# First layer of a hybrid mixer block: queries and keys of the second attention are normed and rotated beside the first attention; inner products of the modulation come later

## The chip, the cores and the metric

One NeuronCore of one Trainium2 chip. The metric is the device time of one execution in microseconds (us); less is better. The engines that matter are PE (TensorE, matmuls and transposes), DVE (VectorE), ACT (ScalarE), POOL (GpSimd, which also starts some DMAs) and SP (which starts the DMAs of weights). Each engine takes its instructions in the order in which the program issued them; between engines only data and buffers order the work.

## The reference, cut to what matters

Two layers over 256 latent and 256 context tokens of width 1024. Each layer normalises and modulates the tokens, multiplies by one wide input matrix, runs three mixers on slices of the result (an mLSTM "ML", a grouped-query attention "GA" with normed and rotated queries and keys, and a neighbourhood attention "NA"), projects, gates and adds them, and ends in a ConvFFN. The second attention's part:

```python
def rms_norm(x, g):
    xf = x.astype(jnp.float32)
    y = xf * lax.rsqrt(jnp.mean(xf * xf, axis=-1, keepdims=True) + EPS)
    return (y * g.astype(jnp.float32)).astype(x.dtype)

def apply_rope(x, cos, sin):
    x1, x2, x3, x4 = jnp.split(x, 4, axis=-1)
    rot = jnp.concatenate([-x2, x1, -x4, x3], axis=-1)
    return x * cos[:, None, :] + rot * sin[:, None, :]

def gqa_qkv(zq, zk, zv, g_q, g_k):          # 8 query heads, 2 key heads of 64
    q = rms_norm(zq.reshape(B, T, GQA_HEADS, HEAD_DIM), g_q)
    k = rms_norm(zk.reshape(B, T, GQA_KV_HEADS, HEAD_DIM), g_k)
    ...

# in reference(), per layer:
mod = (jax.nn.silu(c) @ w_mod[l] + b_mod[l])[:, None, :]
sh1, sc1, ga1, sh2, sc2, ga2 = jnp.split(mod, 6, axis=-1)
...
y_ga = gqa_latent(apply_rope(q_a, cos, sin), apply_rope(k_a, cos, sin), v_a, kc_a, vc_a)
...
x = x + ga1 * rms_norm(o, g_post_mix[l])
f = conv_ffn(modulate(rms_norm(x, g_pre_ffn[l]), sh2, sc2), w_up[l], conv_w[l], conv_b[l], w_down[l])
x = x + ga2 * rms_norm(f, g_post_ffn[l])
```

Only latent tokens are rotated; context keys and queries are normed only. In the second layer the context rows' queries are not needed.

## The kernel before, in words

The kernel is one long list `prog` of pieces. A piece is one chunk of a weight matrix (2 x 128 rows by up to 512 columns) and the matmuls that use it. SP loads the chunk into one of five `raw` buffers; ACT casts it to a high part `whi` (L201), DVE subtracts to get the low part `wlo` (L205), and PE runs three matmul products, high by high and the two crossed ones (L319). `run` goes through the list: a chunk is split up to two pieces ahead of its matmuls, then the piece's matmuls are issued, then `side` steps (one as a rule, two for some pieces) of a queue of Python generators.

These side generators hold everything that isn't a weight matmul, cut at each `yield` into a step. A step's instructions lie on the engines' queues behind the matmuls of its piece. In order, within a layer:

- `g_na` (NA attention) and `g_gqa` (GA attention) end in `g_attend`, which runs in units: a step issues the value matmuls of unit t-2 (L717; ACT casts `yhi` L720, DVE subtracts `ylo` L721), the transposes of unit t-1 (L703, copied to `pT`) and the score matmuls of unit t (L664 for context units, L667 for latent ones), whose softmax DVE and ACT do (L676 to L686).
- ahead of its units, `g_gqa` has nine steps in each layer: the rotation tables (L778, L784); sums of squares and the reciprocal root (L793 to L799, twelve small DVE instructions L117 to L123); then seven steps in which `stage1` (norm and rotation of one 128-token tile: DVE L808, POOL L812 for context and L819 for latent tiles, and one step later DVE L824 and L826) and, three steps behind it, `stage2` (transposes L845 and L850, copies L847 and L851) are staggered. Keys are written twice side by side into a tile `kd`.
- `g_gates` (five steps): gate sums, POOL builds the matrices `GN` (L897 to L900), PE transposes them (L907, L908), later products with the sums L918 to L934.
- `g_mlstm` (mLSTM): `mrow` rows go to DRAM (L949) and come back broadcast as `mb` (L969, function `bcast`), ACT takes exponentials of them (`expo`, L998), DVE multiplies them into score products (L1015), PE forms the outputs (L1028).

PSUM has four banks for weight matmuls and four for side steps. A piece's `need` can force a generator to its end (`finish`).

The order of pieces around the change, layer 0: nq, nk, nv (behind which `g_na` joins the queue), the 272 columns of keys, values and gates (tile `akv`), the GA queries `aq` (piece `attend`, behind which `g_gqa`, `g_gates` and the mLSTM generators join), eight pieces zg(NA), four proj(NA) with two side steps each, eight zg(GA), mk, proj(GA), mq, mv, mo, zg(ML), proj(ML). In layer 1 the order is zg(NA), zg(GA), proj(NA), mk, mq, mv, proj(GA), mo. DVE's evacuation of a projected gate branch, `sig` (L1186), comes at the end of each projected half, with POOL's part L1193 in the later branches.

Between these stand dot pieces (`mod_dot`): one 512 KB chunk of `w_modT` each, which DVE multiplies with the conditioning vector and sums (L451, twice a chunk in layer 0, for latents and context), no PE work and no side step. `spread(a, b, list)` deals such pieces out evenly between two places of `prog`. In layer 0, sixteen of them (`sh2`, `sc2`) lie between `attend` and the last piece of proj(GA) and eight (`ga1`) behind it.

Line numbers in the text and the profile are those of the kernel before.

Of the kernel before, what the change touches and what calls it, by code (L numbers as in the profile page):

```python
# [8 lines left out]
F32 = mybir.dt.float32  # L9
# [4 lines left out]
ALU = mybir.AluOpType  # L14
# [23 lines left out]
class Piece:  # L38
    def __init__(self, raw, emit, k0=0, kn=0, split=True, pre=None, side=1, need=None, share=None, dot=False):
        self.raw, self.emit, self.k0, self.kn, self.split = raw, emit, k0, kn, split  # L40
        self.pre, self.side, self.need = pre, side, need
        self.hi = self.lo = None
        self.dot = dot
        self.hold = self.fence = False
        self.share = share
        if raw:
            raw.left += 1


class Builder:  # L50
# [115 lines left out]
    def run(self):  # L166
        nc = self.nc
        prog = self.prog
        raws = []
        for p in prog:  # L170
            if p.raw and (not raws or raws[-1] is not p.raw):
                raws.append(p.raw)
        state = {"raw": 0, "live": 0, "split": 0}
        RB = 5

        def dma():
            while state["raw"] < len(raws):
# [12 lines left out]
        def use(p):  # L190
            p.raw.left -= 1
            if p.raw.left == 0:
                if p.raw.early:
                    self.u_free(p.raw.tile)
                else:
                    state["live"] -= 1
                dma()

        def split_hi(p):
            p.hi = self.p_w.tile([128, p.kn, p.raw.n], F32R, tag="hi", name="whi")  # L200
            nc.scalar.copy(p.hi, p.raw.tile[:, p.k0:p.k0 + p.kn, :])  # L201

        def split_lo(p):
            p.lo = self.p_w.tile([128, p.kn, p.raw.n], F32R, tag="lo", name="wlo")
            nc.vector.tensor_tensor(p.lo, p.raw.tile[:, p.k0:p.k0 + p.kn, :], p.hi.bitcast(F32), op=ALU.subtract)  # L205
            use(p)

        def split(p):
            if p.split:
                if p.hi is None:  # L210
                    split_hi(p)
                split_lo(p)

        def next_hi():
            q = prog[state["split"]]
            split_hi(q)
            return lambda: split_lo(q)
        self.next_hi = next_hi

        dma()  # L220
        ahead = 0
        for i, p in enumerate(prog):
            if i and prog[i].split and state["split"] > i:
                ahead -= 1
            if p.hold:
                p.need()
                if p.share:
                    state["split"] = i + 1
                split(prog[state["split"]])
                if state["split"] > i:  # L230
                    ahead += 1
                state["split"] += 1
                p.then()
            while state["split"] < len(prog) and state["split"] <= i + 6:
                q = prog[state["split"]]
                if q.hold and state["split"] > i or q.lo is None and state["split"] > i and prog[state["split"] - 1].fence:
                    break
# [12 lines left out]
            if p.need and not p.hold:  # L250
                p.need()
            later, self.later = self.later, []
            if p.share:
                p.emit(p.share.hi, p.share.lo)
            elif p.split:
                p.emit(p.hi, p.lo)
            elif not p.dot:
                p.emit(p.raw.tile)
                use(p)
            for f in later:  # L260
                f()
            for _ in range(p.side):
                self.step()

    def flush(self):
        while self.later:
# [495 lines left out]
        yield from self.g_attend(units, qk, v_of, y)  # L762
        self.u_free(*[st.pop((l, k)) for k in ("nq", "nk", "nv")])

    def g_gqa(self, l):
        nc, st = self.nc, self.st
        AQ, AK = st[l, "aq"], st[l, "akv"]
        qts = [0, 1, 2, 3] if l == 0 else [2, 3]
# [7 lines left out]
        for a in range(2):  # L776
            g = gq[:, a, :]
# [11 lines left out]
        for tt in range(4):  # L789
            if tt in qts:  # L790
                sq = self.t((128, 8, 64), name="sq")
                nc.scalar.activation(out=sq, in_=AQ[:, tt, :].rearrange("p (h d) -> p h d", d=64), func=ACTF.Square)
                nc.vector.tensor_reduce(ssv[:, tt, 0:8], sq, axis=AX.X, op=ALU.add)  # L793
            sk = self.t((128, 2, 64), name="sk")
            nc.scalar.activation(out=sk, in_=AK[:, tt, 16:144].rearrange("p (h d) -> p h d", d=64), func=ACTF.Square)
            nc.vector.tensor_reduce(ssv[:, tt, 8:10], sk, axis=AX.X, op=ALU.add)
        rs = self.sm([128, 40], name="qrs")
        self.rsqrt(rs, ss, 1.0 / 64)
        rsv = rs.rearrange("p (t h) -> p t h", h=10)  # L799
        yield  # L800
        T = 512 if l == 0 else 256
        qT = self.u([128, 4, T], name="qT")
        kT = self.p_l.tile([128, 2, 512], F32, tag="kT", name="kT")
        kd = {}

        def rope(dst, src, nh, r, a, i):

            nc.vector.tensor_tensor(src, src, r.unsqueeze(2).to_broadcast([128, nh, 64]), op=ALU.mult)  # L808
            if i is None:
                g = gq[:, a, :].unsqueeze(1).to_broadcast([128, nh, 64])  # L810
                for d in dst:
                    nc.gpsimd.tensor_tensor(d, src, g, op=ALU.mult)  # L812
                return lambda: None
            t2 = self.t((128, nh, 4, 16), name="t2")
            s4 = src.rearrange("p h (a b c) -> p h a b c", a=2, b=2)
# [6 lines left out]
            def rest():  # L822
                c = tab[:, a, 0, i, :].unsqueeze(1).to_broadcast([128, nh, 64])
                nc.vector.tensor_tensor(src, src, c, op=ALU.mult)  # L824
                for d in dst:
                    nc.vector.tensor_tensor(d, src, t2.rearrange("p h a c -> p h (a c)"), op=ALU.add)  # L826
            return rest

        left = {}

        def stage1(tt):
            i = tt - 2 if tt >= 2 else None
            left[tt] = []
            if tt in qts:
                q = AQ[:, tt, :].rearrange("p (h d) -> p h d", d=64)
                left[tt].append(rope([q], q, 8, rsv[:, tt, 0:8], 0, i))
            k = AK[:, tt, 16:144].rearrange("p (h d) -> p h d", d=64)
            kd[tt] = self.t((128, 2, 2, 64), name="kd")
            left[tt].append(rope([kd[tt][:, :, 0, :], kd[tt][:, :, 1, :]], k, 2, rsv[:, tt, 8:10], 1, i))

        def stage2(tt):
            if tt in qts:
# [6 lines left out]
            for kv in range(2):  # L849
                nc.tensor.transpose(b[:, 128 * kv:128 * kv + 128], kd[tt][:, kv].rearrange("p a d -> p (a d)"), self.I)  # L850
            nc.vector.tensor_copy(kT[:, :, 128 * tt:128 * tt + 128], b[:, 0:256].rearrange("p (a c) -> p a c", a=2))  # L851
        for tt in range(7):
            if tt >= 3:
                stage2(tt - 3)
            if 1 <= tt <= 4:
                for f in left.pop(tt - 1):
                    f()
            if tt < 4:
                stage1(tt)
            yield  # L860
        self.u_free(st.pop((l, "aq")))
        y = self.y_alloc(l, GA)
# [252 lines left out]
    def layer(self, l):  # L1115
# [126 lines left out]
        in_T("nk", C_NK, allT, None, need=None if L0 else lambda: self.finish("c2c"))  # L1242
        in_nat("nv", C_NV, [0, 1, 2, 3], ev_v("nv"), after=lambda: self.add_side(self.g_na(l), "na"))
        valued = self.prog[-1]
        self.block(cols(C_A, 272), 8, 272, "nat", [0, 1, 2, 3], X, ev_kv)
        self.block(cols(C_A + 272), 8, 512, "nat", tl, X, ev_q,
                   after=lambda: (self.add_side(self.g_gqa(l), "gqa"), self.add_side(self.g_gates(l), "gates"),
                                  self.add_side(self.g_mlstm(l)), self.add_side(self.g_mlfin(l))))
        attend = self.prog[-1]
        if L0:  # L1250
            zg(NA, 0)
            zg(NA, 1)
        else:
            zg(NA, 1)
            zg(GA, 0)
            zg(GA, 1)
        proj(NA, 0, need=lambda: self.finish("na"))
        if L0:

            for p in self.prog[-4:]:  # L1260
                p.side = 2
            zg(GA, 0)
            zg(GA, 1)
        in_T("mk", C_MK, allT, 128 ** -0.5)
# [17 lines left out]
        stop = self.prog[stop]  # L1282

        if L0:
            a, b = self.prog.index(attend), self.prog.index(mlstm)
            self.spread(a, b, [p for k in ("sh2", "sc2") for p in self.mod_dot(0, k)])
            a = self.prog.index(mlstm)
            self.spread(a + 2, self.prog.index(first), self.mod_dot(0, "ga1"))

        if not L0:  # L1290

# [308 lines left out]
```

## Time and profile before

| | us |
|---|---|
| median of 3 runs | 1506.92 (1506.75 to 1507.0) |
| the profiled execution | 1506.16 |
| its span in the profile | 1504.4 |

The mean granted clock of PE in the profiled execution is 0.988 of full speed. The costliest groups are the three matmul products L319 (464.5, 459.9 and 459.6 us for the largest form of each), the subtraction L205 on DVE (413.3 us in 330 instructions) and the cast L201 on ACT (335.8 us). The dots L451 take 157.4 us of DVE.

How to read it: PE's busy share says how much of the span is matmul; what is not busy is waiting, and the view of waits says for which engine and line. The granted clock (PEclk) tells where the throttle ran PE at half speed, which doesn't show as idle time. Where a time is given as a place (242.87 us), it counts from the start of the span.

### The profile page before, as it was taken

The page shows a single profiled execution, that of the slowest core. Times are in us where ns is not written, and L with a number is a line of the kernel's source. Part 1 is how long each engine was busy: PE and PEld are TensorE (multiplying, and loading weights), DVE is VectorE, ACT ScalarE, POOL GpSimd, SP SyncE. Part 2 cuts the span into 40 slices and gives each one's busy share as a digit, 9 for nine tenths or more (in the row PEclk, how much of TensorE's full clock was granted, in tenths as well). Part 3 has the DMA queues.
Part 4 walks back from the last instruction along what each step waited for, and adds up shares of the span by engine and source line. Part 5 has one row for each costly group of instructions (what it writes and reads, how often), then busy time and mean ns, then how long its engine had stood idle before and what let it go on. Part 6 is the DMA issues. An engine that isn't in the chain of part 4 may idle for free.

```text
span 1504.4 us, 22921 instructions
## 1 busy us (share of the span) xinstructions
PE 1442.5 (96%) x8681; PEld 1251.2 (83%) x8681; DVE 1073.0 (71%) x1872; ACT 730.8 (49%) x1343; POOL 212.4 (14%) x312
## 2 busy tenths in 40 slices
PE   6999998999999999799999999999999899899997
PEld 3877786778888889788888888887978789799986
DVE  4438788776846578988887787738896556778874
ACT  3434443443455357433444566535544355566663
POOL 2000021002520121111111010100200330312100
PEclk9999999999999999999999999999999999999999
DMA  9623333333642356555454777634454545455662
GB/s 336 199 78 121 102 127 98 90 102 104 175 134 78 98 183 195 182 182 170 146 178 136 236 234 247 222 120 125 141 166 143 192 96 169 154 182 184 209 207 88
DMA packets 103806, 238.07 MB, mean 158 GB/s; under 512 B 8416, under 2 KB 18720, under 8 KB 103568
## 3 DMA queue, kind: packets, MB, share of 16 engines
q1 hardware_dynamic: 99472, 224.56, 46.8%
q0 software_dynamic: 4224, 12.05, 3.0%
q8 instruction: 68, 1.11, 0.3%
q14 instruction: 42, 0.34, 0.1%
HBM read 235.50 MB, written 1.08 MB: 157 GB/s over the span
## 4 chain that ended last, share of the span: by engine, by line
PE 82%; DVE 8%; ACT 3%; issue 3%; POOL 2%; DMA 1%; SPq 0%; DVEq 0%; POOLq 0%; ACTq 0%
PE bank L319 68%; PE bank L703 3%; PE bank L717 3%; PE bank L667 2%; PE bank L1028 2%; DVE wlo L205 2%; DVE ta L1359 1%; DVE jnk L451 1%; PE bank L421 1%; PE bank L664 1%; ACT whi L201 1%; PE bank L1005 1%; DMA raw<-in_w_mod 1%; DMA mb<-mrow 1%; POOL t L819 1%
## 5 line engine op out<-in xcount | busy, mean ns | idle before, releaser
L205 DVE TENSOR_TENSOR wlo<-raw,whi 128x1024 fp32r<-128x1024 f32 (+1 forms) x330 | 413.3, 1265 | 162.3 <-ACT whi L201 160.8
L319 PE MATMUL bank<-HThi,whi 128*128 128x256 f32 (+1 forms) x1408 | 464.5, 330 | 8.8 <-DVE ta L1359 4.5
L319 PE MATMUL bank<-HThi,wlo 128*128 128x256 f32 (+1 forms) x1408 | 459.9, 327 | 7.2 <-DVE wlo L205 7.0
L319 PE MATMUL bank<-HTlo,whi 128*128 128x256 f32 (+1 forms) x1408 | 459.6, 326 | 0.5 <-DVE HTlo L586 0.5
L201 ACT CAST whi<-raw 128x1024 fp32r<-128x1024 f32 (+1 forms) x330 | 335.8, 1037 | 175.1 <-PE bank L319 126.4
L319 PEld LDWEIGHTS bank<-HThi,whi 128*128 128x128 f32 x1408 | 270.2, 192 | 40.4 <-issue 15.5
L319 PEld LDWEIGHTS bank<-HThi,wlo 128*128 128x128 f32 x1408 | 270.2, 192 | 26.8 <-DVE wlo L205 8.7
L319 PEld LDWEIGHTS bank<-HTlo,whi 128*128 128x128 f32 x1408 | 270.5, 192 | 18.7 <-DVE HTlo L586 1.2
L319 PE MATMUL bank<-whi,xs 128*128 128x512 f32 x528 | 159.9, 381 | 0.9 <-DVE ta L1359 0.8
L451 DVE SCALAR_TENSOR_TENSOR jnk<-raw,CB 128x1024 bf16<-128x1024 f32 x128 | 157.4, 1229 | 1.8
L319 PE MATMUL bank<-whi,HThi 128*128 128x512 f32 (+1 forms) x384 | 142.5, 371 | 0.0
L1359 DVE SCALAR_TENSOR_TENSOR ta<-bank,cw,ta 128x255 f32<-128x255 f32 (+2 forms) x224 | 110.7, 527 | 41.7 <-ACT ta L1356 37.6
L319 PE MATMUL bank<-wlo,HThi 128*128 128x512 f32 (+1 forms) x384 | 139.1, 362 | 0.0
L319 PE MATMUL bank<-whi,HTlo 128*128 128x512 f32 (+1 forms) x384 | 139.1, 362 | 0.0
L319 PEld LDWEIGHTS bank<-whi,xs 128*128 128x128 f32 x528 | 99.8, 189 | 16.6 <-ACT ta L1378 1.3
L1356 ACT ACTIVATE ta<-bank,cw 128x256 f32<-128x256 f32 (+1 forms) x96 | 61.2, 646 | 101.9 <-PE bank L319 100.2
L679 ACT ACTIVATE pr<-bank,mn 128x512 f32<-128x512 f32 (+1 forms) x96 | 58.5, 614 | 89.0 <-DVE mn L676 80.6
L1379 POOL TENSOR_TENSOR hT<-ta 128x256 f32<-128x256 f32 (+1 forms) x48 | 56.6, 1182 | 309.3 <-ACT ta L1378 309.0
L319 PE MATMUL bank<-wlo,xs 128*128 128x512 f32 x264 | 100.1, 379 | 0.0
L319 PEld LDWEIGHTS bank<-whi,HThi 128*128 128x128 f32 x384 | 72.6, 189 | 20.4 <-issue 10.9
L319 PEld LDWEIGHTS bank<-whi,HTlo 128*128 128x128 f32 x384 | 72.6, 189 | 8.6
L319 PEld LDWEIGHTS bank<-wlo,HThi 128*128 128x128 f32 x384 | 72.6, 189 | 8.0
(228 smaller groups left out, 1728.9 us busy)
## 6 DMA issues: line engine op xcount, KB each, us to landing
raw<-in_w_in SPq DMA_DIRECT2D x112, 512.0 KB, 3.9
raw<-in_w_up SPq DMA_DIRECT2D x96, 512.0 KB, 4.6
raw<-in_w_modT SPq DMA_DIRECT2D x80, 512.0 KB, 4.2
raw<-in_w_down SPq DMA_DIRECT2D x66, 512.0 KB, 4.6
raw<-in_w_branch SPq DMA_DIRECT2D x24, 512.0 KB, 4.0
raw<-in_w_out SPq DMA_DIRECT2D x24, 512.0 KB, 4.2
raw<-in_w_mod SPq DMA_DIRECT2D x16, 512.0 KB, 10.5
nab<-in_nabias POOLq DMA_DIRECT2D x16, 256.0 KB, 4.1
```

Source lines behind the costliest of these rows:

```text
L201: nc.scalar.copy(p.hi, p.raw.tile[:, p.k0:p.k0 + p.kn, :])
L205: nc.vector.tensor_tensor(p.lo, p.raw.tile[:, p.k0:p.k0 + p.kn, :], p.hi.bitcast(F32), op=ALU.subtract)
L319: nc.tensor.matmul(out, l, self.woven(r), start=first and i == 0, stop=last and i == 2)
L451: nc.vector.scalar_tensor_tensor(self.jnk, rt[:, 0, :], 1.0, self.CB[:, s, :], op0=ALU.mult, op1=ALU.mult, accum_out=dst[:, j, s:s + 1])
L667: nc.tensor.matmul(b, q[:, c0:c0 + 128], k[:, 0:512], start=True, stop=True)
L679: nc.scalar.activation(out=pt[:, w * i:w * i + w], in_=b[:, w * i:w * i + w], func=ACTF.Exp, scale=-1.0, bias=mn[:, i:i + 1], accum_out=mn ...
L703: nc.tensor.transpose(b[:, o:o + 128], pt[:, 128 * i:128 * i + 128], self.I)
L717: nc.tensor.matmul(b[64 * par:64 * par + 64, 0:w], v_of(p, par, kt), pTs[par][:, w * kt:w * kt + w], start=kt == 0, stop=kt == nkt - 1)
L1028: nc.tensor.matmul(b[:, d, 0:129], v[:, o:o + 128], V[:, s, h, :], start=n == 0, stop=n == len(sl) - 1)
L1356: nc.scalar.activation(out=tv, in_=bv, func=ACTF.Identity, scale=cw[:, ch, 1:2], bias=cw[:, ch, 3:4])
L1359: nc.vector.scalar_tensor_tensor(o, x, cw[:, ch, t:t + 1], o, op0=ALU.mult, op1=ALU.add)
L1379: nc.gpsimd.tensor_tensor(hv, av, ta, op=ALU.mult)
```

## The change

1. The first half of `g_gqa` (tables, squares, roots, norm and rotation) becomes a generator of its own, `g_prep`. It works in place: keys are rotated in `akv`, and DVE copies them into `kd` later. The squares are in two steps of two tiles each.
2. In layer 0 the nine pieces of `attend` and zg(NA) get `also`: each advances `g_prep` by one step besides its own side step, which belongs to `g_na`. In layer 1 `g_gqa` runs `g_prep` first, as part of its own steps.
3. `g_gqa` then has five steps (copy to `kd`, transposes, copies) ahead of its attention units. In layer 0 that makes 5 in place of 9, and proj(NA) pieces go back to one side step. In layer 1 it makes 12 in place of 9, and what follows in the queue starts three steps later.
4. The 24 dot pieces of layer 0 are dealt out in one go, `ga1` first, from `attend` + 13 (zg(GA)) to the fourth piece behind the first of mo.

```diff
-    def g_gqa(self, l):
+    def g_prep(self, l):
@@ Builder.run
             for _ in range(p.side):
                 self.step()
+            if p.also:
+                next(p.also(), None)
@@ g_prep, squares of tile tt
             nc.vector.tensor_reduce(ssv[:, tt, 8:10], sk, axis=AX.X, op=ALU.add)
+            if tt == 1:
+                yield
...
-                for d in dst:
-                    nc.gpsimd.tensor_tensor(d, src, g, op=ALU.mult)
+                nc.gpsimd.tensor_tensor(src, src, gq[:, a, :].unsqueeze(1).to_broadcast([128, nh, 64]), op=ALU.mult)
...
-                for d in dst:
-                    nc.vector.tensor_tensor(d, src, t2.rearrange("p h a c -> p h (a c)"), op=ALU.add)
+                nc.vector.tensor_tensor(src, src, t2.rearrange("p h a c -> p h (a c)"), op=ALU.add)
             return rest
-        left = {}
-        def stage1(tt):
+        left = []
+        for tt in range(4):
             i = tt - 2 if tt >= 2 else None
-            left[tt] = []
+            more = []
             if tt in qts:
+                more.append(rope(AQ[:, tt, :].rearrange("p (h d) -> p h d", d=64), 8, rsv[:, tt, 0:8], 0, i))
+            more.append(rope(AK[:, tt, 16:144].rearrange("p (h d) -> p h d", d=64), 2, rsv[:, tt, 8:10], 1, i))
+            for f in left:
+                f()
+            left = more
+            yield
+        for f in left:
+            f()
+    def g_gqa(self, l):
+        prep = st.pop("prep")
+        if l:
+            yield from prep
+        for _ in prep:
+            pass
...
-        for tt in range(7):
-            if tt >= 3:
-                stage2(tt - 3)
-            if 1 <= tt <= 4:
-                for f in left.pop(tt - 1):
-                    f()
+        for tt in range(5):
+            if tt:
+                stage2(tt - 1)
             if tt < 4:
-                stage1(tt)
+                kd[tt] = self.t((128, 2, 2, 64), name="kd")
+                k = AK[:, tt, 16:144].rearrange("p (h d) -> p h d", d=64)
+                nc.vector.tensor_copy(kd[tt], k.unsqueeze(2).to_broadcast([128, 2, 2, 64]))
             yield
@@ order of pieces
-        self.block(cols(C_A, 272), 8, 272, "nat", [0, 1, 2, 3], X, ev_kv)
+        self.block(cols(C_A, 272), 8, 272, "nat", [0, 1, 2, 3], X, ev_kv, after=lambda: st.update(prep=self.g_prep(l)))
         if L0:
+            first = len(self.prog) - 1
             zg(NA, 0)
             zg(NA, 1)
+            for p in self.prog[first:]:
+                p.also = lambda: st.get("prep", iter(()))
...
         if L0:
-            for p in self.prog[-4:]:
-                p.side = 2
             zg(GA, 0)
             zg(GA, 1)
...
         if L0:
-            a, b = self.prog.index(attend), self.prog.index(mlstm)
-            self.spread(a, b, [p for k in ("sh2", "sc2") for p in self.mod_dot(0, k)])
-            a = self.prog.index(mlstm)
-            self.spread(a + 2, self.prog.index(first), self.mod_dot(0, "ga1"))
+            self.spread(self.prog.index(attend) + 13, self.prog.index(first) + 4,
+                        [p for k in ("ga1", "sh2", "sc2") for p in self.mod_dot(0, k)])
```

Where the rows stand, at three places. In the rows of the changed kernel the lines are its own: 2 higher up to the generators and 14 higher behind them (L205 stays, L453 is L451, L678 is L676, L723 is L721, L865 is L851, L873 is the copy to `kd`, L905 is L891, L938 is L924, L948 is L934, L1012 is L998, L1147 is L1133, L1162 is L1148, L1200 is L1186).

First, DVE around the first proj(NA) pieces of layer 0. Before:

```order
223 L451 SCALAR_TENSOR_TENSOR jnk,sh_1181<-raw,CB 128x1024 x2
224 L1186 SCALAR_TENSOR_TENSOR sig<-sig,bank 128x512 x4
225 L462 TENSOR_TENSOR sh_1181<-sh_1181,bcol 128x16
226 L851 COPY kT<-bank 128x2x128
227 L824 TENSOR_TENSOR aq<-aq,tab 128x512
228 L826 TENSOR_TENSOR aq<-aq,t_2054 128x512
229 L824 TENSOR_TENSOR akv<-akv,tab 128x128
230 L826 TENSOR_TENSOR kd<-akv,t_2059 128x2x64 x2
231 L808 TENSOR_TENSOR aq<-aq,qrs 128x512
232 L808 TENSOR_TENSOR akv<-akv,qrs 128x128
233 L851 COPY kT<-bank 128x2x128
234 L824 TENSOR_TENSOR aq<-aq,tab 128x512
```

Now:

```order
227 L865 COPY kT<-bank 128x2x128
228 L873 COPY kd<-akv 128x256
229 L205 TENSOR_TENSOR wlo<-raw,whi 128x1024
230 L865 COPY kT<-bank 128x2x128
231 L873 COPY kd<-akv 128x256
232 L205 TENSOR_TENSOR wlo<-raw,whi 128x1024
233 L453 SCALAR_TENSOR_TENSOR jnk,ga_2088<-raw,CB 128x1024 x2
234 L1200 SCALAR_TENSOR_TENSOR sig<-sig,bank 128x512 x4
235 L865 COPY kT<-bank 128x2x128
236 L205 TENSOR_TENSOR wlo<-raw,whi 128x1024
237 L678 TENSOR_REDUCE mn<-bank 128x1 x2
```

The norm and the rotation (L808, L824, L826) are gone from here; the copies to `kd` and the transposed keys remain, with one dot between casts, and the first scores of the attention (L678) follow.

Second, DVE beside a context unit of `g_na` in layer 0 (the piece is one of zg(NA)). Before:

```order
165 L684 RECIPROCAL rc<-mn 128x2
166 L686 TENSOR_SCALAR pr<-pr,rc 128x256 x2
167 L684 RECIPROCAL rc<-mn 128x2
168 L686 TENSOR_SCALAR pr<-pr,rc 128x256 x2
169 L205 TENSOR_TENSOR wlo<-raw,whi 128x1024
170 L451 SCALAR_TENSOR_TENSOR jnk,sh_1181<-raw,CB 128x1024 x2
171 L721 TENSOR_TENSOR ylo<-bank,yhi 128x256
172 L708 COPY pT<-bank 128x512
```

Now:

```order
184 L122 SCALAR_TENSOR_TENSOR rs_b<-rs_b,rs_a 128x40
185 L123 SCALAR_TENSOR_TENSOR qrs<-rs_b,qrs 128x40
186 L121 TENSOR_TENSOR rs_b<-qrs 128x40
187 L122 SCALAR_TENSOR_TENSOR rs_b<-rs_b,rs_a 128x40
188 L123 SCALAR_TENSOR_TENSOR qrs<-rs_b,qrs 128x40
189 L121 TENSOR_TENSOR rs_b<-qrs 128x40
190 L122 SCALAR_TENSOR_TENSOR rs_b<-rs_b,rs_a 128x40
191 L123 SCALAR_TENSOR_TENSOR qrs<-rs_b,qrs 128x40
192 L205 TENSOR_TENSOR wlo<-raw,whi 128x1024
193 L723 TENSOR_TENSOR ylo<-bank,yhi 128x256
194 L710 COPY pT<-bank 128x512
195 L678 TENSOR_REDUCE mn<-bank 128x2 x2
```

The dot (L451) between `wlo` and `ylo` is gone; the last eight of prep's root instructions stand ahead of `wlo`, with the other four and two tiles' sums of squares above them.

Third, ACT in layer 1 from the gates (E) to the first exponentials of the mLSTM (`mq` and `mv` are evacuations of those pieces, `cm` and `MB` are steps of the gates, `D<-mb` waits for the broadcast). Before:

```order
507 L890 ACTIVATE E<-E 128x32
508 L891 ACT_TABLE_LOAD
509 L891 ACTIVATE E<-E 128x32
510 L201 CAST whi<-raw 128x1024 x3
511 L1133 COPY mq<-bank 128x256 x4
512 L924 COPY cm<-bank 128x512
513 L201 CAST whi<-raw 128x1024
514 L934 COPY MB<-bank 128x512
515 L940 ACT_TABLE_LOAD
516 L940 ACTIVATE em<-em 128x32
517 L201 CAST whi<-raw 128x1024 x2
518 L998 ACTIVATE D_11052<-mb,gc 128x256
```

Now:

```order
511 L904 ACTIVATE E<-E 128x32
512 L905 ACT_TABLE_LOAD
513 L905 ACTIVATE E<-E 128x32
514 L201 CAST whi<-raw 128x1024 x3
515 L938 COPY cm<-bank 128x512
516 L201 CAST whi<-raw 128x1024
517 L1162 COPY mv<-bank 128x4x128 x4
518 L948 COPY MB<-bank 128x512
519 L954 ACT_TABLE_LOAD
520 L954 ACTIVATE em<-em 128x32
521 L201 CAST whi<-raw 128x1024
522 L1012 ACTIVATE D_11120<-mb,gc 128x256
```

The evacuation of `mq` has moved ahead of E and that of `mv` ahead of `MB`; the exponentials come right behind `em` and one cast, where two casts stood between.

More of the change, by code (lines that the diff above doesn't have):

```diff
@@ L41, in __init__ @@
         self.pre, self.side, self.need = pre, side, need
-        self.hi = self.lo = None
+        self.hi = self.lo = self.also = None
         self.dot = dot
@@ L800, in g_gqa, with rope @@
         yield
[L801 to L806, printed above, removed]
+        def rope(src, nh, r, a, i):
             nc.vector.tensor_tensor(src, src, r.unsqueeze(2).to_broadcast([128, nh, 64]), op=ALU.mult)
             if i is None:
-                g = gq[:, a, :].unsqueeze(1).to_broadcast([128, nh, 64])
-                for d in dst:
-                    nc.gpsimd.tensor_tensor(d, src, g, op=ALU.mult)
+                nc.gpsimd.tensor_tensor(src, src, gq[:, a, :].unsqueeze(1).to_broadcast([128, nh, 64]), op=ALU.mult)
                 return lambda: None
@@ L824, in rest @@
                 nc.vector.tensor_tensor(src, src, c, op=ALU.mult)
-                for d in dst:
-                    nc.vector.tensor_tensor(d, src, t2.rearrange("p h a c -> p h (a c)"), op=ALU.add)
-            return rest
-        left = {}
-        def stage1(tt):
+                nc.vector.tensor_tensor(src, src, t2.rearrange("p h a c -> p h (a c)"), op=ALU.add)
+            return rest
+        left = []
+        for tt in range(4):
             i = tt - 2 if tt >= 2 else None
-            left[tt] = []
+            more = []
             if tt in qts:
[L835 to L839, printed above, removed]
+                more.append(rope(AQ[:, tt, :].rearrange("p (h d) -> p h d", d=64), 8, rsv[:, tt, 0:8], 0, i))
[7 more added lines that the diff above has]
+    def g_gqa(self, l):
+        nc, st = self.nc, self.st
+        qts = [0, 1, 2, 3] if l == 0 else [2, 3]
+        prep = st.pop("prep")
[3 more added lines that the diff above has]
+            pass
+        AQ, AK = st[l, "aq"], st[l, "akv"]
+        T = 512 if l == 0 else 256
+        qT = self.u([128, 4, T], name="qT")
+        kT = self.p_l.tile([128, 2, 512], F32, tag="kT", name="kT")
+        kd = {}
         def stage2(tt):
```

## The prediction

> **What bounds the kernel now.** I read the page first, then the chain of waits, then busy time by stage.
>
> ```profile
> span 1504.4 us, 22921 instructions
> PE 1442.5 (96%) x8681; PEld 1251.2 (83%) x8681; DVE 1073.0 (71%) x1872; ACT 730.8 (49%) x1343; POOL 212.4 (14%) x312
> PE 82%; DVE 8%; ACT 3%; issue 3%; POOL 2%; DMA 1%; SPq 0%; DVEq 0%; POOLq 0%; ACTq 0%
> ```
>
> PE is the bound. The change takes no matmul away, so all it can win is PE idle time and half-clock time. By stage in layer 0 (window, length, then PE, PEld, DVE, ACT, POOL busy, clock, DMA):
>
> ```profile
> 64.00:225.00 161.00, 159.85 (x908) 129.82 (x907) 104.63 (x211) 67.47 (x144) 10.86 (x13) 1.00 0.34 104
> 225.00:256.00 31.00, 24.45 (x112) 18.65 (x111) 26.15 (x50) 8.65 (x16) 6.47 (x9) 0.89 0.29 85
> 256.00:340.00 84.00, 84.00 (x515) 64.86 (x514) 60.48 (x119) 37.96 (x94) 1.09 (x2) 1.00 0.33 101
> ```
>
> PE is full before and after 225 to 256 us; there it idles 31.00 - 24.45 = 6.55 us. This is where proj(NA), with two side steps a piece, runs the first half of g_gqa. The waits of PE in that window, and its timeline:
>
> ```profile
> PE bank L703 <- DVE pr L686: 3.1, 1, 3.1
> PE bank L845 <- DVE aq L826: 1.9, 1, 1.9
> PE bank L319 <- ACT whi L201: 1.4, 1, 1.4
> ```
>
> ```profile
> 242.87 1.13 PE L667 MATMUL bank<-kT,qT 64*128 64x512 f32 x4
> 247.12 1.97 PE L703 MATMUL bank<-ident,pr 128*128 128x128 f32 x8 [3.13 <-DVE pr L686]
> 249.02 2.08 PE L667 MATMUL bank<-kT,qT 64*128 64x512 f32 x4
> ...
> 252.89 0.41 PE L319 MATMUL bank<-HTlo,whi 128*128 128x512 f32 x1
> ```
>
> After the 3.13 us gap the same four L667 take 2.08 instead of 1.13 us, until 252.89: 5.8 us at half clock, 2.8 us lost. All three waits end on DVE, whose rows are:
>
> ```profile
> 227.80 2.47 DVE L1186 SCALAR_TENSOR_TENSOR sig<-sig,bank 128x512 f32<-128x512 f32 x4
> ...
> 232.66 0.69 DVE L808 TENSOR_TENSOR aq<-aq,qrs 128x512 f32<-128x512 f32 x1
> ...
> 233.47 0.42 DVE L851 COPY kT<-bank 128x256 f32<-128x256 f32 x1
> 234.95 0.80 DVE L824 TENSOR_TENSOR aq<-aq,tab 128x512 f32<-128x512 f32 x1 [1.06 <-POOL t L819]
> ...
> 242.46 2.47 DVE L1186 SCALAR_TENSOR_TENSOR sig<-sig,bank 128x512 f32<-128x512 f32 x4
> ```
>
> Two proj pieces put rotation, tile copies, two dots and 2.47 us of L1186 in a row on DVE, and rotation waits for POOL's product L819.
>
> **Layer 0: what goes.** With prep finished beside the nine pieces of attend and zg(NA), transposes L845 read finished tiles, so the 1.9 goes; one step per proj piece and no rotation leave L1186 (2.47) alone between two pieces, so the 1.4 and the 3.1 go, and with them the 2.8. Gain 6.55 + 2.8 = **9.3 us**. What comes back:
>
> ```profile
> 209.96 0.68 DVE L793 TENSOR_REDUCE qss<-sq 128x8 f32<-128x512 f32 x1
> 210.55 0.28 DVE L796 TENSOR_REDUCE qss<-sk 128x2 f32<-128x128 f32 x1
> 210.86 0.18 DVE L117 TENSOR_SCALAR rs_a<-qss 128x40 f32<-128x40 f32 x1
> ...
> 213.39 0.20 DVE L123 SCALAR_TENSOR_TENSOR qrs<-rs_b,qrs 128x40 f32<-128x40 f32 x1
> ...
> 218.99 1.77 DVE L808 TENSOR_TENSOR aq<-aq,qrs 128x512 f32<-128x512 f32 x1
> ```
>
> - *Prep beside g_na.* The third prep step is the heaviest: 2 x (0.68 + 0.28) of reduces and twelve rsqrt instructions, 210.86 to 213.59 = 2.7, together 4.6 us. The others lie at 1.5 to 2.7 (rotation of a tile: 0.69 + 0.28, and as much twice for the rest). What an attention unit bears is seen where a dot (two L451, 2.6 us) stands in it now: the score matmuls take 1.32 instead of 1.14 us, then ylo follows the dot at once.
>
> ```profile
> 159.04 1.14 PE L664 MATMUL bank<-nk,nq 64*128 64x256 f32 x8
> ...
> 167.53 1.32 PE L664 MATMUL bank<-nk,nq 64*128 64x256 f32 x8
> ```
>
> ```profile
> 167.38 0.29 DVE L721 TENSOR_TENSOR ylo<-bank,yhi 128x128 fp32r<-128x128 f32 x1
> ```
>
>   So 2.6 us fits at about 0.2, and of the third step 4.6 - 2.6 = 2.0 does not; part is taken by banks in hand. Between 0 and 2.0 I take 1.2. Dots leave this stretch: -0.5 for two or three such 0.2s.
> - *kd.* Four copies of 128x256 replace the doubled write; the nearest row is kT's copy of the same size, 0.42 (233.47, above), so 0.4 each. The first stands ahead of the first transposes: from 0 to three such, 1.2; I take 0.5.
> - *Dots closer together.* 24 in some 28 pieces where 16 stood: a 0.2 to 0.4 at one or two context units and 0.5 at the GN matrices (POOL copies beside DVE): 0.8, from 0 to 3.
>
> Layer 0: 9.3 - 1.2 - 0.5 - 0.8 + 0.5 = **7.3 us gained** (4.5 to 9).
>
> **Layer 1: what moves.** The words of the change name layer 0, but g_gqa is now 12 + 10 steps in layer 1 instead of 9 + 10, so g_gates and g_mlstm come three pieces later.
>
> *Gates.* The block of 16 GN matmul pairs, layer 0 then layer 1, one wait, and POOL:
>
> ```profile
> 361.20:364.90 3.70, 3.70 (x34) 3.65 (x33) 0.69 (x1) 0.00 (x0) 3.70 (x4) 1.00 0.06 20
> 1165.60:1176.85 11.25, 6.89 (x37) 6.21 (x36) 5.15 (x8) 1.23 (x2) 6.54 (x14) 0.75 0.68 234
> ```
>
> ```profile
> PE bank L908 <- POOL GN L899: 2.9, 2, 2.2
> ```
>
> ```profile
> 1168.36 1.20 POOL L900 COPY GN<-F 128x4 f32<-128x4 f32 x1
> ```
>
> In layer 1 the block costs 11.25 against 3.70: 7.5 us more, and the tail of half clock behind it some 1.4 (estimated): 8.9. Now a whole mv piece (128x512 matmuls) lies between F and GN where an mq piece (128x256) lay: PE comes 2.5 us later, and of 4.4 us of waiting 1 to 2 stays. Gain **7.4** (2 to 9).
>
> *mLSTM.* g_mlstm now starts on proj(GA) pieces with two steps each, where bcast(0) (the broadcast DMA of rows through DRAM) and expo(0) (the exps that need it) fall in one piece.
>
> ```profile
> 1189.90:1249.40 59.50, 56.16 (x351) 51.42 (x350) 32.86 (x96) 31.69 (x76) 19.06 (x38) 0.97 0.49 129
> ```
>
> ```profile
> 1190.34 0.59 ACT L934 COPY MB<-bank 128x512 f32<-128x512 f32 x1 [4.76 <-PE bank L930]
> ...
> 1198.80 0.91 ACT L998 ACTIVATE D<-mb,gc 128x256 f32<-128x256 f32 x2 [4.44 <-DMA mb<-mrow]
> ```
>
> ```profile
> 1219.03 1.41 DVE L1186 SCALAR_TENSOR_TENSOR sig<-sig,bank 128x256 f32<-128x256 f32 x4
> 1220.35 2.46 DVE L1015 TENSOR_TENSOR D<-D,bank 128x256 f32<-128x256 f32 x8
> ```
>
> ```profile
> 1228.56 1.53 PE L1007 MATMUL bank<-mq,mk 128*128 128x256 f32 x4 [2.60 <-DVE H L1039]
> ```
>
> From MB's copy to the first exp is 8.46 us whatever PE does meanwhile (two DMAs through DRAM). Before, two mv pieces lay in it; now ACT stands in expo(0) with the next casts queued behind. In us from MB: exps 8.5 to 12, cast and wlo to 14.2, L1186 1.41 to 15.6, eight L1015 2.46 to 18; PE wants the products at 9.6 (three proj pieces of some 2.6 and the scores between, an estimate), and its 3 us of L1028 end near 19.8 instead of 12.6: 7.2 stalled. The second broadcast is issued behind POOL's sigmoid adds: about 3.5 more, then 1.5. Sum 12.2. Before, this stretch idled 59.50 - 56.16 = 3.3 and lost 0.03 x 59.5 = 1.8 to the clock: 5.1. Loss **7.1** (0 to 11).
>
> The attention of layer 1: 0 (-1.5 to 1.5); its prep still goes in the same generator.
>
> **Sum:** 7.3 + 7.4 - 7.1 = 7.6; I take 0.5 off for half-clock windows that new gaps may open: 7.1. Against its own time 1506.16 that is 1499.1. The profiled run stands 0.76 below the median of 1506.92, so 1499.8 on the median's scale.
>
> **The Trainium skill against the rows.** Half clock sets in here at 245.9, after a gap of 3.13 us, and a gap of 1.9 ahead of it left the clock whole. The Trainium skill, "TensorE: Matmul & The Clock Gate", section "HAM oscillation — how this bites in real kernels", has the rule that idle gaps of more than about 3.4 us halve it; by that the 3.13 would not have halved it, layer 0 would gain 2.8 less and the sum be 1502.6; the trace disagrees, and it decides. The second: L808 takes 0.69 us alone and 1.77 beside POOL's L812. The Trainium skill, "GPSIMD Engine Reference", section "8. Key points", says that GpSimd shares its SBUF interfaces with VectorE and contends with instructions of two SBUF inputs; the trace agrees, and it speaks against prep's POOL products beside attention: were each of three rotation units 1.5 us over the 2.6 that a unit bears, the sum would be 1504.3. I give that a part of rival 3.
>
> **Rivals.**
> 1. *The mLSTM start is hidden.* If expo(0) holds nothing that PE needs, the 7.1 is 0: 1506.9 - 7.3 - 7.4 + 0.5 = 1492.7. For it: PE has the proj pieces' casts ahead of it; against: ACT runs in order. 0.12.
> 2. *Layer 1 keeps its GN wait.* POOL's copies at 1.2 stay contended, PE stands half as long and drops to half clock again: the gain is 2 instead of 7.4: 1506.9 - 7.3 - 2 + 7.1 = 1504.7. 0.17.
> 3. *The change doesn't do what it says:* the wait only moves, since POOL's products end late or prep's leftovers run at the first step of g_gqa. Layer 0 gains 2.5, the rest comes to +0.2: 1504.6. 0.12.
> 4. *Slower: the dots.* DVE is busy 60.48 of 84 us in 256 to 340 with some six dots; with nine it is 68 of 84, but units are chains, with gaps it can't use. The point: when a unit's DVE work exceeds PE's 8.5 us (159.04 to 167.53 in the rows of L664). If 24 pieces come 0.5 late each, +12: 1499.8 + 12 = 1511.8. Against: dots fit at 0.2 now. 0.06.
>
> **Numbers.** My forecast holds 0.53. The range 1495 to 1505 takes in rivals 2 and 3 and the bounds of layer 0; rival 1 and rival 4 stay out, with 0.02 of tails. A measurement of this kernel tells about 0.2% (3 us) from no change: faster means below 1503.9, slower above 1509.9. Nearly all of the forecast, rival 1 and half of 2 and 3 are faster: 0.80. Within: 0.14. Slower: 0.06.
>
> **What would show it.** Right: no wait of PE above 1 us in proj(NA), clock 1.00 there; one wait of about 1 us in zg(NA) behind the rsqrt; a GN block near 5 us in layer 1; ACT idle some 5 us on the DMA mb in proj(GA) and L1028 waiting for D behind it. Wrong: L845 still waiting for DVE, ylo late in each GA unit, or no wait on mb at all.

## The result, and the profile after

The changed kernel takes **1499.48 us** (median of 4 runs, 1497.83 to 1499.66), the kernel before 1506.96 (4 runs, 1506.75 to 1507.04): a ratio of 0.9946 with a 95% interval of 0.9934 to 0.9958. That is 7.5 us less; the forecast was 1499.8. The profiled execution took 1499.34 us, against 1506.16 before. The number was right; its terms were not all, and this part is about them. Among the executions of the experiments below, one of e4 (7885 us) and one of e10 (5258 us, the one with the trace) took several times as long as the others, and medians and ratios leave them out.

From the page of the changed kernel:

```profile
PE 1439.5 (96%) x8681; PEld 1248.9 (83%) x8681; DVE 1072.5 (72%) x1876; ACT 730.8 (49%) x1343; POOL 214.4 (14%) x308
```

```profile
PE 85%; DVE 7%; ACT 3%; DMA 2%; issue 2%; POOL 2%; SPq 0%; DVEq 0%; POOLq 0%; ACTq 0%
```

PE's share of the chain that ended last is 85% instead of 82%, and that of DMA 2% instead of 1%: less of the end is set by other engines, a little more by transfers (the broadcast of the mLSTM is one of them, below).

To see where the time went, I take two matmuls that stand at the same place of both programs and that wait for the same thing in all kernels: the first transposes of layer 1's first attention (place Q) and the transposes ahead of its FFN (place R). Before, then after, from the timelines of PE:

```profile
1015.77 1.33 PE L703 MATMUL bank<-ident,pr 128*128 128x128 f32 x8 [1.14 <-DVE pr L686]
...
1314.80 1.94 PE L534 MATMUL bank<-ident,xn 128*128 128x128 f32 x8 [4.77 <-DVE xn L515]
```

```profile
1007.46 1.33 PE L705 MATMUL bank<-ident,pr 128*128 128x128 f32 x8 [1.14 <-DVE pr L688]
...
1308.33 1.94 PE L536 MATMUL bank<-ident,xn 128*128 128x128 f32 x8 [4.78 <-DVE xn L517]
```

Up to Q, where all lies that the change does in layer 0, 8.31 us are won. From Q to R, 299.03 us have become 300.87: layer 1 gives 1.84 back. These are single executions, and the same code doesn't reach Q and R at the same time in each (below), so a term is known no better than to some 2 us.

Layer 0 after, by stage; the second row is the stretch of proj(NA), which was 225 to 256 before:

```profile
130.00:394.50 264.50, 262.51 (x1479) 210.90 (x1478) 196.38 (x387) 112.92 (x247) 43.95 (x68) 1.00 0.36 111
215.00:246.00 31.00, 30.85 (x152) 25.37 (x151) 21.38 (x38) 9.93 (x18) 0.00 (x0) 1.00 0.34 106
```

In proj(NA) PE idles 0.15 us instead of 6.55, at full clock instead of 0.89. The three waits are gone, and POOL has nothing to do there. The one wait of layer 0 that is left between 130 and 394.5 us stands near mq:

```profile
392.26 1.98 PE L1019 MATMUL bank<-mq,mk 128*128 128x512 f32 x4 [1.74 <-ACT mq L1147]
```

Layer 1 after, the waits of PE from 1060 to 1260 us:

```profile
PE bank L1042 <- DVE D L1029: 5.1, 1, 5.1
PE bank L864 <- DVE kd L873: 2.7, 1, 2.7
PE bank L705 <- DVE rc L686: 2.0, 1, 2.0
PE bank L321 <- DVE wlo L205: 1.7, 2, 1.3
PE bank L1021 <- DVE H L1053: 1.0, 1, 1.0
...
```

and its stages (attention, GN block, mLSTM):

```profile
1060.00:1130.00 70.00, 64.00 (x474) 56.30 (x474) 59.24 (x118) 28.38 (x54) 10.68 (x11) 0.95 0.56 177
1177.60:1181.30 3.70, 3.70 (x33) 3.59 (x32) 0.39 (x4) 0.14 (x1) 1.41 (x9) 1.00 0.93 314
1196.00:1240.00 44.00, 37.49 (x247) 34.54 (x246) 23.06 (x68) 24.16 (x62) 20.21 (x37) 0.92 0.44 102
```

No wait for GN is in the list any more, and the GN block takes 3.70 us, as in layer 0, where it took 11.25. In its place stand the late product D (5.1) and three waits in the attention (2.7, 2.0 and 1.3), 6.0 us idle of 70 and a clock of 0.95. The forecast had nothing for those three.

### The profile page after: what moved, and what is told of

It is laid out like the page before. It is cut to its first block, busy times and chain, and to the rows that moved or that the text cites. A ratio compares the mean times of both kernels' runs of the same rounds, so it can differ in the third digit from the quotient of the medians.

```text
span 1497.6 us, 22906 instructions
## 1 busy us (share of the span) xinstructions
PE 1439.5 (96%) x8681; PEld 1248.9 (83%) x8681; DVE 1072.5 (72%) x1876; ACT 730.8 (49%) x1343; POOL 214.4 (14%) x308
## 4 chain that ended last, share of the span: by engine, by line
PE 85%; DVE 7%; ACT 3%; DMA 2%; issue 2%; POOL 2%; SPq 0%; DVEq 0%; POOLq 0%; ACTq 0%
PE bank L321 70%; PE bank L705 3%; PE bank L719 3%; PE bank L669 3%; DVE wlo L205 2%; PE bank L1042 2%; DVE ta L1371 1%; DMA mb<-mrow 1%; PE bank L423 1%; ACT D L1012 1%; PE bank L666 1%; DMA raw<-in_w_mod 1%; DVE jnk L453 1%; ACT whi L201 1%; POOL sig L1207 1%
## 5 line engine op out<-in xcount | busy, mean ns | idle before, releaser
L205 DVE TENSOR_TENSOR wlo<-raw,whi 128x1024 fp32r<-128x1024 f32 (+1 forms) x330 | 411.9, 1261 | 162.9 <-ACT whi L201 161.9
L453 DVE SCALAR_TENSOR_TENSOR jnk<-raw,CB 128x1024 bf16<-128x1024 f32 x128 | 156.6, 1224 | 1.8
```

Source lines behind the costliest of these rows:

```text
L453: nc.vector.scalar_tensor_tensor(self.jnk, rt[:, 0, :], 1.0, self.CB[:, s, :], op0=ALU.mult, op1=ALU.mult, accum_out=dst[:, j, s:s + 1])
```

## The experiments

On the three chips of the experiments the kernel before scatters more (1503.2 to 1510.3; medians 1507.24 for e1 to e4, 1508.05 for e5 to e8, 1507.71 for e9 to e11) than on the first, and so do the others; ratios are to the kernel before on the same chip. The traces scatter too: the seven executions with the layer 0 of the change have Q at 1004.49 to 1007.46, and the four with the old layer 1 throughout (before, e1, e3, e9) take 298.98 to 300.69 from Q to R. So a difference of 1 to 3 us counts only where waits of the trace go with it. The places Q and R of each profiled execution, in us:

| kernel | median us | ratio (95%) | Q | Q to R |
|---|---|---|---|---|
| before | 1506.96 | | 1015.77 | 299.03 |
| the change | 1499.48 | 0.9946 (0.9934 to 0.9958) | 1007.46 | 300.87 |
| e1_layer0_only | 1496.92 | 0.9941 (0.992 to 0.9963) | 1005.43 | 298.98 |
| e2_gates_later | 1504.03 | 0.998 (0.997 to 0.9989) | 1014.57 | 295.36 |
| e3_dots_only | 1504.51 | 0.9989 (0.9978 to 1.0) | 1012.49 | 300.69 |
| e4_dots_old | 1504.32 | 0.9976 (0.9964 to 0.9989) | 1009.14 | 300.05 |
| e5_two_steps | 1492.92 | 0.9895 (0.9881 to 0.991) | 1006.40 | 292.48 |
| e6_lead | 1493.75 | 0.9908 (0.9892 to 0.9925) | 1006.50 | 294.03 |
| e7_eleven | 1496.22 | 0.992 (0.9901 to 0.994) | 1004.49 | 297.47 |
| e8_again (the change) | 1498.82 | 0.9937 (0.9921 to 0.9952) | 1007.18 | 301.08 |
| e9_single | 1507.23 | 0.9999 (0.9989 to 1.0009) | 1021.20 | 299.17 |
| e10_gap3 | 1490.69 | 0.9898 (0.9879 to 0.9917) | not used | not used |
| e11_gap2 | 1491.19 | 0.9898 (0.9881 to 0.9914) | 1006.96 | 292.14 |

**Layer 0 alone.** Layer 1 gets the old function back, as g_gqa_old:

```diff
-                   after=lambda: (self.add_side(self.g_gqa(l), "gqa"), ...
+                   after=lambda: (self.add_side(self.g_gqa(l) if L0 else self.g_gqa_old(l), "gqa"), ...
```

> The change in layer 0 only; layer 1 runs the nine staggered steps of g_gqa as before. Theory A (from where the two traces stand apart at the same weight matmul: 8.3 us at the end of layer 0, 6.8 at the end): layer 1 as changed loses 1.5 net, so this kernel is about 8.3 us below before, near 1498.6, with the GN wait of about 4.4 us in layer 1 back. Theory B (the forecast): layer 0 gains 7.3 and layer 1 next to nothing, 1499.6. Theory C: layer 1's shift is a clear gain (GN wait gone), this kernel is 3 us or more slower than the changed one, 1502 or more.

1496.92, and from Q to R 298.98, as before. What the change is meant to do in layer 0 is all of its gain, and theory C falls. That layer 1 as changed costs more isn't shown: from Q to R it takes 300.87, 301.08 and 300.05 us (the change, e8, e4), the old one 299.03, 298.98, 300.69 and 299.17 (before, e1, e3, e9). The means are 1.2 us apart, less than the spread of the old one, and by times the two kernels can't be told apart either (0.9941 and 0.9946, the intervals overlap).

**The gates later, nothing else.** The kernel before with

```diff
     def g_gates(self, l):
         nc, st = self.nc, self.st
+        if l:
+            for _ in range(3):
+                yield
```

> The kernel before, with three empty steps ahead of the gates of layer 1: gates and mLSTM stand where the change puts them, the attentions as before. Theory A: the GN block is worth 9 us, the later mLSTM start costs 4, the attention stays as before: 1506.9 - 9 + 4 = 1502. Theory B (the forecast's sizes): 7.4 gained, 7.1 lost, 1506.6. Theory C: the new gaps of layer 1's attention (2.7 and 2.0 us) come from what follows it in the queue, so they show here too: 1508 or more.

1504.03, ratio 0.998: 3 us faster, and 3.67 less from Q to R. Theory A had 5, theory B 0.3. PE's waits in layer 1:

```profile
PE bank L1031 <- DVE D L1018: 4.5, 1, 4.5
...
PE bank L911 <- POOL GN L902: 1.4, 1, 1.4
PE bank L703 <- DVE rc L684: 1.0, 1, 1.0
```

The late D is there (4.5), one GN wait of 1.4 is left of 4.4, and the attention has only its old 1.0. So theory C falls: the attention's new waits are not from what follows it. What the GN block costs is seen in 30 us around it, before and in e2:

```profile
1160.00:1190.00 30.00, 24.81 (x168) 23.40 (x167) 17.41 (x33) 7.50 (x12) 10.05 (x23) 0.89 0.53 176
```

```profile
1172.00:1202.00 30.00, 28.63 (x186) 26.43 (x185) 15.48 (x36) 10.10 (x15) 12.81 (x29) 1.00 0.48 156
```

Before, 5.2 us are idle and 0.11 of 30 us, some 3.3, lost to the clock: 8.5. In e2 it is the 1.4 of the wait. The block gives 8.5 - 1.4 = 7.1, and 3.67 stays, so the later mLSTM start costs some 3.4 (estimated). Both are nearer to theory A's sizes (9 and 4) than to theory B's (7.4 and 7.1).

**The dots apart.** The 24 dot pieces dealt as in the change, in the kernel before; and the changed kernel with the old dealing:

```diff
e3:  kernel before
-    self.spread(a, b, [p for k in ("sh2", "sc2") ...]) and self.spread(a + 2, ..., self.mod_dot(0, "ga1"))
+    self.spread(self.prog.index(attend) + 13, self.prog.index(first) + 4, [p for k in ("ga1", "sh2", "sc2") ...])
e4:  changed kernel, the same lines the other way round
```

> The kernel before, with the 24 dot pieces of layer 0 dealt out as in the change, nothing else. Theory A: dots aren't what stalls proj(NA): 1 us gained beside the first attention, 1 to 2 lost near mq, 1506 to 1508, and the waits of 1.9 and 3.1 us in proj(NA) stay. Theory B: dots between the rotation's instructions make that stall: 4 us or more gained, 1503 or less.

> The changed kernel with the 24 dot pieces where they stood before (sixteen from the first attention on). Theory A: dots (2.6 us of DVE) and prep steps (up to 4.6) meet beside the first attention's units and overrun what a unit bears three or four times by 1 to 2.5 us, the mq gap of 1.7 goes: about 1499.5 + 4 - 1.5 = 1502. Theory B: units have room for both, 1498.

With the dots alone Q comes at 1012.49, 3.3 us earlier than before, with 2.4 and 1.7 of the old waits in proj(NA) still there, as theory A has it; the time lies between the two theories' numbers. With prep alone Q comes at 1009.14, 6.6 earlier than before and 1.7 later than with the change, in an execution 4 us faster than the median of e4; the ratio is 0.9976: A. The wait that it adds in layer 0:

```profile
PE bank L864 <- DVE kd L873: 2.6, 1, 2.6
```

```profile
204.49 1.76 DVE L453 SCALAR_TENSOR_TENSOR jnk<-raw,CB 128x1024 bf16<-128x1024 f32 x1
...
212.95 0.29 DVE L824 TENSOR_TENSOR akv<-akv,t 128x128 f32<-128x128 f32 x1
213.16 0.28 DVE L873 COPY kd<-akv 128x256 f32<-128x256 f32 x1
```

With a dot on DVE beside the rotation, the whole rotation is late, the copy to kd behind it, and PE waits for that copy. Dots and prep want the same room beside the first attention. Prep alone has the larger part of what is won at Q, and dealing the dots out later takes this wait away.

**The same places, a longer lead.** e1 with three empty steps behind the staggered nine, so that attention units, gates and mLSTM of layer 1 stand where the change has them:

```diff
                 stage1(tt)
             yield
+        for _ in range(3):
+            yield
```

> As the changed kernel in every place of attention units, gates and mLSTM (layer 1's g_gqa has twelve steps), but layer 1's norm and rotation are the nine staggered steps of before, followed by three empty ones. Theory A (the waits of 1.3 and 2.7 us in layer 1's attention come from transposing kd one step behind a copy that stands behind the whole rotation on DVE): both waits go and 4 to 5 us of the changed kernel's time with them, 1494 to 1495. Theory B (the waits come from the later place of the units): within 1 us of the changed kernel.

1493.75 (0.9908), 6.8 us less from Q to R than the change; A, and somewhat more than it expected. PE's waits there, and the stage of the attention:

```profile
PE bank L1158 <- DVE D L1145: 4.9, 1, 4.9
PE bank L705 <- DVE pr L688: 1.8, 1, 1.8
PE bank L1137 <- DVE H L1169: 1.2, 1, 1.2
PE bank L321 <- DVE wlo L205: 1.0, 3, 0.4
...
```

```profile
1060.00:1130.00 70.00, 67.69 (x510) 59.05 (x509) 61.10 (x120) 30.24 (x57) 11.45 (x13) 1.00 0.57 187
```

The wait for kd and the 1.3 for wlo are gone; the one for the softmax (1.8, against 2.0) stays with the place of the units, and so does the late D. Against the change, where the same 70 us had 64.00 busy at clock 0.95, 3.7 us of idle time have gone and some 3.5 of half clock, which theory A had not counted.

**One step fewer in layer 1.** The squares in one step there, so gates and mLSTM are two pieces later than before, not three:

```diff
-            if tt == 1:
+            if tt == 1 and l == 0:
```

> The changed kernel with layer 1's sums of squares in one step (eleven steps of g_gqa in layer 1 instead of twelve): gates and mLSTM two pieces later than before, not three. Theory A: GN wait still gone, the mLSTM start has its mv piece back, 3 to 4 us better than the changed kernel; the attention's stalls stay: 1496. Theory B: the third piece makes no difference, 1499.5; or the GN wait comes back, 1503.

> The changed kernel itself on this chip, beside the others: 1499.5 if chips agree; on the earlier chip of these experiments the kernel before scattered from 1503 to 1510, so some us of scatter.

1496.22 against 1498.82 for the change itself on the same chip (the intervals of the ratios overlap), 3.6 less from Q to R. That is theory A's number, but only in part by its terms. PE's waits from 1160 to 1230:

```profile
PE bank L1021 <- DVE H L1053: 1.7, 1, 1.7
PE bank L1042 <- DVE D L1029: 1.3, 2, 1.1
PE bank L921 <- POOL GN L913: 0.9, 1, 0.9
PE bank L922 <- POOL GN L913: 0.8, 1, 0.8
```

One mv piece between the broadcast and the exps takes the 5.1 down to 1.1, as A has it. But 1.7 of the wait for GN is back, and the attention, whose stalls were to stay, has the wait for kd without any half clock:

```profile
1078.27 0.44 PE L864 MATMUL bank<-ident,kd 128*128 128x128 f32 x2 [2.66 <-DVE kd L873]
```

```profile
1058.00:1128.00 70.00, 65.31 (x511) 56.82 (x509) 61.66 (x122) 29.69 (x58) 10.68 (x11) 1.00 0.56 179
```

So a part of e7's gain is the clock of the attention, 1.00 where the change has 0.95.

**Both together, and better than both.** e1 with two empty steps ahead of layer 1's gates (e5); with an empty step between broadcast and exps besides (e11); and with three and one (e10):

```diff
+        if l:
+            for _ in range(2):      # e10: 3
+                yield
...
         bcast(0)
         yield
+        if l:                       # e10 and e11
+            yield
         expo(0)
```

> The change in layer 0, layer 1's g_gqa as before, and two empty steps ahead of layer 1's gates, so that POOL's GN matrices get the longer mv piece and the mLSTM broadcast keeps a mv piece between its DMA and the exps. Theory A (GN block worth some 8 to 9 us, mLSTM loss only where the exps come right behind the broadcast): 1497 - 8 + 1 = 1490. Theory B (any later start of the mLSTM costs what the GN block gives): 1495 to 1497.

> As e5_two_steps (two empty steps ahead of layer 1's gates) with one empty step between the mLSTM's broadcast and its exps. Theory A: the remaining 1.1 and 1.7 us waits in the mLSTM shrink, up to 2 us less than e5_two_steps, 1491. Theory B: those waits are from later broadcasts, behind POOL's sigmoid sums, and the extra step changes nothing or costs 1 at the end: 1493 to 1494.

> As e5_two_steps with three empty steps ahead of layer 1's gates and one more between the mLSTM's broadcast DMA and its exps. Theory A (ACT's queue behind the wait for the broadcast is what makes the 5 us gap): GN wait 0 instead of 1.7, no gap above 3 us at the first outputs, 1490 to 1492. Theory B (the data come late whatever stands behind them): gap of 4 us or more at the outputs, 1494.

1492.92, 1491.19 and 1490.69, ratios 0.9895, 0.9898 and 0.9898: the three are not told apart, and their intervals lie below that of the change (0.9921 to 0.9952, e8). These are the fastest of all, 15 to 17 us below the kernel before on their chips. e5 takes 8.4 us less from Q to R than the change: A, 3 us short of its number. The mLSTM's waits in e5, then in e11:

```profile
PE bank L1138 <- DVE H L1170: 1.7, 1, 1.7
PE bank L1159 <- DVE D L1146: 1.2, 2, 1.1
```

```profile
PE bank L1138 <- DVE H L1170: 2.6, 1, 2.6
...
PE bank L1159 <- DVE D L1146: 0.3, 1, 0.3
```

The extra step takes the wait for D from 1.2 to 0.3, and the wait for H grows from 1.7 to 2.6. ACT's half of H stands behind the exps of the second broadcast, which POOL issues behind the sigmoid sums (L1326 is L1193 of before, L1129 is L998):

```profile
1199.17 2.79 POOL L1326 TENSOR_TENSOR sig<-sig 128x256 f32<-128x256 f32 x4 [4.02 <-DVE sig L1319]
1201.91 1.09 POOL L1100 DMA_DIRECT2D mb<-mrow  x2
```

```profile
1205.81 0.91 ACT L1129 ACTIVATE D<-mb,gc 128x256 f32<-128x256 f32 x2 [7.36 <-DMA mb<-mrow]
```

That is theory B's mechanism; 1491.19 is the number of theory A, but e11's ratio is that of e5, and from Q to R it takes only 0.34 less. Of e10 only the times are used, so whether the gap at the outputs closed there isn't known.

**Single steps without the move.** The kernel before with one side step per proj(NA) piece:

```diff
-            for p in self.prog[-4:]:
-                p.side = 2
```

> The kernel before with one side step on each proj(NA) piece of layer 0 instead of two; prep is not moved, dots stay. Theory A (two steps a piece are half of the stall; the other half is the room that the nine steps take, since 23 steps then meet 19 pieces and four units run in a row ahead of proj(GA)): the waits of proj(NA) shrink by some 5 us with their half clock, but four units in a row without weight matmuls cost 12 us or more: 1510 or more. Theory B (the double steps alone are the cause, the move of prep isn't needed): 1500.

1507.23, ratio 0.9999: between the theories. The profiled execution, with its late Q, is the slowest of the ten (1511.66). Of proj(NA)'s waits one of 1.1 and one of 0.3 are left, and six new ones stand ahead of proj(GA), where the last units run in a row without weight matmuls (42 us with 37.44 busy, clock 0.96):

```profile
330.00:372.00 42.00, 37.44 (x219) 28.96 (x215) 27.43 (x56) 14.14 (x39) 9.92 (x24) 0.96 0.18 57
```

```profile
PE bank L703 <- DVE pr L686: 4.6, 6, 1.5
```

Taking the double steps away only moves the stall. That the four steps which prep takes out of the queue are what pays fits with e4, which has single steps, the old dots and prep moved, at a ratio of 0.9976 and Q at 1009.14. My 12 us for that row of units was too much: it is 4.6 of idle time and some 1.7 of half clock (0.04 of 42).

## Why the prediction was right, and where it was not

| term | forecast us | measured us |
|---|---|---|
| layer 0 | -7.3 | -8.3 (-7.1 to -11.3 over the executions with either layer 0) |
| GN block of layer 1 | -7.4 | -8.5 |
| mLSTM start of layer 1 | +7.1 | about +3.4 (from e2) |
| attention of layer 1 | 0 (-1.5 to 1.5) | +5.1 to +6.8 (from e6) |

- **Proj(NA).** Right: all three waits are gone, and the idle 6.4 of 6.55 us with them. Of the 9.3, the half clock's 2.8 is not a fixed cost: e2 runs the same layer 0 with the same three waits (3.1, 1.9 and 1.4) at full clock,

```profile
225.00:256.00 31.00, 24.38 (x135) 1.00 0.32 95
```

  and its Q comes 1.2 us earlier than before's. The prediction has the half clock set in behind the gap of 3.13 us. By the granted clock it sets in within the gap: PE stands idle from 244.0 to 247.12, and the clock is 1.00 up to 246.0 and 0.50 from 246.2 to 252.7.
- **The third prep step.** 1.2 was too dear. It runs 4.4 us on DVE, and the unit that bears it has score matmuls of 1.49 instead of 1.14 us; from its transposes to the next ones are 8.84 us, where the unit ahead took 8.48:

```profile
173.86 1.09 PE L705 MATMUL bank<-ident,pr 128*128 128x128 f32 x8
174.88 1.14 PE L666 MATMUL bank<-nk,nq 64*128 64x256 f32 x8
182.34 1.09 PE L705 MATMUL bank<-ident,pr 128*128 128x128 f32 x8
183.37 1.49 PE L666 MATMUL bank<-nk,nq 64*128 64x256 f32 x8
191.18 1.09 PE L705 MATMUL bank<-ident,pr 128*128 128x128 f32 x8
```

  so 0.36 more, about what a dot of 2.6 us costs there. The wait of about 1 us behind the roots that was named as a sign isn't there. DVE takes the step early in the unit, when its softmax is done, and the idle time ahead of ylo (2.15 us in a unit of the kernel before) bears it.
- **kd in layer 0.** 0.5 was put down, none is seen. That holds only because the dots have left: e4 has 2.6 there.
- **Dots.** The price of 0.8 can't be checked to that size: the mq wait, 0.45 before and 1.74 after, is 2.05 in e2, whose layer 0 is that of before. The dots' leaving seems worth more than the 0.5 of the forecast: 1.7 at Q beside prep, with one wait of 2.6 gone.
- **GN in layer 1.** Right that three pieces of delay take the wait, and it went wholly, where 1 to 2 was to stay, with the half clock behind it: 7.55 by the block's own time (11.25 to 3.70), 8.5 with the idle time and half clock of the 30 us around it.
- **mLSTM.** The chain was right: ACT stands 4.31 us for the broadcast with the cast behind it, then exps, cast, L1200, L1029, and PE's outputs:

```profile
1195.86 0.59 ACT L948 COPY MB<-bank 128x512 f32<-128x512 f32 x1 [0.53 <-PE bank L944]
...
1203.23 0.91 ACT L1012 ACTIVATE D<-mb,gc 128x256 f32<-128x256 f32 x2 [4.31 <-DMA mb<-mrow]
```

  MB to first exp is 7.37 us, not 8.46, and the gap 5.1, not 7.2; the second is 1.0 where 3.5 was put down.
- **The step that failed** is "The attention of layer 1: 0 (-1.5 to 1.5); its prep still goes in the same generator." In layer 1 the generator has the same work, but no longer the same lead. Before, the norm of tile tt stood three steps ahead of its transposes, and kd was written with the rotation, at least two steps ahead. Now all four tiles are rotated first, and the copy to kd stands one step (one zg piece) ahead of its transposes, behind all of DVE's rotations:

```profile
1084.55 0.29 DVE L824 TENSOR_TENSOR akv<-akv,t 128x128 f32<-128x128 f32 x1
1084.76 0.29 DVE L873 COPY kd<-akv 128x256 f32<-128x256 f32 x1
```

```profile
1085.10 0.47 PE L864 MATMUL bank<-ident,kd 128*128 128x128 f32 x2 [2.67 <-DVE kd L873]
```

  The copy takes 0.29 us; what PE waits for is the queue ahead of it. e6 shows the price: with the old stagger, at the same places, 6.8 us less from Q to R, and 5.1 less by the medians. About half of the 6.8 is half clock, which the change has in all three of its traces (0.95 in the change, e8 and e4) and e7, with the same wait for kd, has not; the idle time alone is 3.7. I had worked the copy out for layer 0 alone, and none of the four rivals had it either.

The terms as measured, with 6.8 for the attention (e6) and 3.4 for the mLSTM (e2): -8.3 - 8.5 + 3.4 + 6.8 = -6.6; the difference at R is -6.5 (1314.80 to 1308.33). With the scatter of the traces, so close an agreement is partly chance. The forecast's sum came out by luck: the mLSTM was 3.7 us too dear and layer 0 and GN some 2 too cheap, and the missed attention cost about as much as both.

## What to carry to other kernels

Where a step is split in two, look at the lead that each result keeps over its reader in every place that runs the code, not only where the change is meant: the copy of 0.29 us brought a wait of 2.67 by its place in a queue. Count the steps of a shared queue in each layer; three more of them moved everything behind, took one wait away and made another. A stage that waits for a round trip through DRAM wants something long between the issue and the first reader on an engine that takes its instructions in order.

## What the runs showed of the hardware

Half clock doesn't follow from the length of a gap alone. The 3.46 us wait in layer 0's FFN is there in two executions of the changed kernel, 3.46 and 3.44, and the clock of the 60 us around it is 0.97 in one and 0.94 in the other (the change, then e8). In the kernel before the same wait, 3.46, goes with 1.00 (third row):

```profile
600.00:660.00 60.00, 54.05 (x324) 0.97 0.58 186
```

```profile
600.00:660.00 60.00, 54.07 (x321) 0.94 0.57 182
```

```profile
600.00:660.00 60.00, 50.91 (x339) 1.00 0.57 183
```

0.03 and 0.06 of 60 us lost at half speed are some 3.6 and 7.2 us of half clock (estimated). The Trainium skill, "TensorE: Matmul & The Clock Gate", section "What's actually happening", says that the activity window is about 3.4 us long and runs freely, so that the moment depends on where in it the work lands. These rows agree, and so do the proj(NA) gaps of before and e2, 3.13 us each, with and without half clock. A limit of 3.4 us for a single gap doesn't hold in these traces, either way: 3.46 left the clock whole in the kernel before, while the 3.13 there and the 2.67 of the change came with half clock. A difference of 1 to 3 us between two kernels with gaps of 2 us or more may be no more than this.
